# Hybrid encoder layer, one core: mLSTM gates and values beside the second HGRN pair, queries and keys behind it

## The chip, the cores and the metric

The kernel runs on one core of one Trainium2 chip. The metric is the time of one execution on the device in microseconds (us). The core's engines are named as the profile names them: PE (TensorE, matrix multiplication) with PEld (its weight loads), DVE (VectorE), ACT (ScalarE), POOL (GpSimd) and SP (SyncE, which issues most of the DMAs). Each engine works through its own queue of instructions in order; engines wait for each other by semaphores.

## What is computed

One encoder layer over 512 tokens of width 1024, in float32. Its first part, where the change lies, projects the normalised tokens once to 4624 columns and feeds four HGRN heads and four mLSTM heads of 128 columns each, both scanned forward and backward:

```python
(h_q, h_f_fwd, h_f_bwd, h_i, h_g,
 m_q, m_k, m_v, m_o,
 m_ig_fwd, m_ig_bwd, m_fg_fwd, m_fg_bwd) = split_cols(proj, IN_SPLITS)
...
o_h = hgrn2_scan(q_h, k_fwd, v_h, lf_fwd) + flip_seq(hgrn2_scan(flipped ...))
hgrn_out = head_rmsnorm(o_h, hgrn_g) * silu(h_g)
qk = silu(centred_dwconv(concat(m_q, m_k), conv_w, conv_b))        # width 5
...
h_m = mlstm_scan(q_m, k_m, v_m, ig_fwd, lfg_fwd) + flip_seq(mlstm_scan(flipped ...))
mlstm_out = head_rmsnorm(h_m, mlstm_g) * sigmoid(m_o)
x = x + concat(hgrn_out, mlstm_out) @ w_out
x = x + cross_attention(rmsnorm(x), rmsnorm(mem), ...)             # 256 memory tokens
x = x + relu(rmsnorm(x) @ w_up) ** 2 @ w_down
return rmsnorm(x, norm_final)
```

## The kernel before

Every projection of float32 values is made of three fp32r matmuls (`mm3`, L235 to L238): each operand is split into a high part (ACT copies it, L232) and a low part (DVE subtracts, L233), and high x high, high x low and low x high are added in PSUM. A block of weights, 128 x 1024, is loaded by SP into one of three `st` tiles, split into `wh` and `wl` (three tiles each), and used for 24 matmuls. The order of the blocks is the list SEQ (`_split_order`), and the splits run two blocks ahead of their use.

Projections are generators that emit a matmul group and then call `tick()` (L189), which gives one step to one of the running chains; `rate[0]` is how many steps a tick gives. `proj_d` ticks after every 12 matmuls, `proj_t` after 12 (two tiles). So chains are woven between the projection matmuls of PE's queue. The final order on each engine is made by a scheduler that knows priorities; the weight splits have a high one.

The chains around the change:

- `hgrn_pair(p)` (L359): two HGRN heads. It goes through seven levels (1, 2, 4 to 64). At each, PE computes 32 small score matmuls (L384), then DVE updates queries (L476), keys (L479) and gates (L483) of both heads and takes the scores into the matrix under a mask (L414), and ACT combines keys (L393). The next level's scores need these. After a level the chain yields `pace[0]` times, so that many ticks go by before the next. Behind the levels come L430 and L431 (products across 128 tokens), L443 and L445, and the values (L454).
- `head_out` (L486), the norm of a head: squares on ACT (L492), mean on DVE (L172), power -0.5 on POOL (L174), product on DVE (L494), then four transposes on PE (L501), the gate (L502) and a split.
- `qk_proj(p)` (L726): the projection of two heads' queries and keys, and for each of the four tiles the convolution (`conv_evac`): ACT adds the bias (L639), DVE multiplies and adds five taps (L643, four of L645), ACT takes the sigmoid (L647), DVE multiplies (L650).
- `mlstm_chain(h)` (L653): per direction a row broadcast on PE (L659), DVE adds a mask (L662), ACT writes ten exponentials of 128 x 128 (L669); then four score matmuls in full fp32 (L673), DVE multiplies (L676, L678), and the sums over tokens (L688) with the reciprocals and scalings (L694 to L701); then `head_out`.

The exponential and the sigmoid lie in different tables of ACT; where the queue changes between them, an ACT_TABLE_LOAD stands in it.

The main program projects the first pair's columns and starts it, projects the second pair's beside it, ends the first pair's levels, starts the second pair, and projects beside that: queries and keys of the first two mLSTM heads, mLSTM values (`mv_proj`, 3584), output gates (`gate_proj`, 4096 and 4352). Then the memory tokens are normed, transposed and split (L780, L783, L784), the second two heads' queries and keys are projected, and the mLSTM chains run beside the memory's keys and values (blocks of 256 columns) and the start of the output projection.

Of the kernel before, what the change touches and what calls it, by code (L numbers as in the profile page):

```python
# [33 lines left out]
V_MQK, V_MO, V_GATE = 40, 48, 52  # L34
# [11 lines left out]
def _split_order():  # L46
    def d(m, c0, n):
        return [("d", m, 0, c0 + P * i) for i in range(n)]

    def t(m, k0, c0, n=4):  # L50
        return [("t", m, k0 + 2 * i, c0) for i in range(n)]

    seq = t("in", 0, 1536) + [("d", "gate", 0, 0)]
    for g in (0, 512, 1024, 2048):
        seq += d("in", g, 2)
    for g in (0, 512, 1024):
        seq += d("in", g + 256, 2)
    seq += d("in", 2304, 2) + d("in", 2560, 2) + d("in", 3072, 2)
    seq += t("in", 0, 3584) + d("in", 4096, 2) + d("in", 4352, 2)
    seq += d("in", 2816, 2) + d("in", 3328, 2)  # L60
    seq += d("kv", 0, 8) + t("kv", 0, 1024) + t("kv", 0, 1536)
    seq += t("out", 0, 0) + t("out", 0, 512)
    seq += d("xq", 0, 8)
    seq += t("xo", 0, 0) + t("xo", 0, 512)
    for f in range(4):
        for j in range(4):
            seq += d("up", 1024 * f + P * j, 1) + d("up", 1024 * f + P * (j + 4), 1)
        seq += [("t", "down", 8 * f + 2 * g + k, 0) for g in range(2) for k in (0, 4)]
        seq += [("t", "down", 8 * f + 2 * g + 4, 512) for g in range(2)]
    seq += [("t", "down", 8 * f + 2 * g, 512) for f in range(4) for g in range(2)]  # L70
    return seq


SEQ = _split_order()
SIDX = {key: i for i, key in enumerate(SEQ)}
NSTREAM = len(SEQ) - 8
# [3 lines left out]
def trunk(ctx: ExitStack, tc: tile.TileContext, x, mem, wpk, vec, cst, lmask, rmask, rows, out):  # L80
# [12 lines left out]
    def T(tag, w, bufs, dt=F32):  # L93
        return (sb if w == 516 else big).tile([P, w], dt, tag=tag, name=nm(tag), bufs=bufs)
# [4 lines left out]
    def smb():  # L99
        return pss.tile([P, 512], F32, tag="sm", name=nm("sm"))  # L100

    def tiny(w):
        return sb.tile([P, w], F32, tag=f"tiny{w}", name=nm("tiny"), bufs=2 if w == 8 else 6)
# [9 lines left out]
    RG = lambda: T("rg", 1024, 1)  # L113
# [56 lines left out]
    def rstd_of(ss, w, n):  # L170
        ms = tiny(w)
        v.tensor_scalar(out=ms, in0=ss, scalar1=1.0 / n, scalar2=EPS, op0=ALU.mult, op1=ALU.add)  # L172
        r = tiny(w)
        gp.tensor_tensor(out=r, in0=ms, in1=nh.to_broadcast([P, w]), op=ALU.pow)  # L174
        return r, ms
# [11 lines left out]
    def tick1():  # L187
        if chains:
            turn[0] += 1  # L189
            g = chains[turn[0] % min(2, len(chains))]  # L190
            try:
                next(g)
            except StopIteration:
                chains.remove(g)
# [5 lines left out]
    def until_scored(p):  # L200
        while p not in scored:
            tick1()
# [46 lines left out]
    def proj_d(mat, c0, xs, n=512, count=2):  # L249

        for j in range(count):
            wh, wl = weights(("d", mat, 0, c0 + P * j))
            ps = mmb()
            for k in range(8):
                z = slice(k * P, k * P + P)
                mm3(ps[:, :n], wh[:, z], wl[:, z], xs[k][0], xs[k][1], k == 0, k == 7)
                if k == 3:
                    tick()
            yield ps
            tick()  # L260
# [65 lines left out]
    for t, ps in proj_t("in", 0, 1536, xs):  # L326
        d = VV()
# [306 lines left out]
    def conv_evac(h, isk, ps):  # L634
        c = (4 if isk else 0) + h
        pad = T2()
        gp.memset(pad[:, 0:2], 0.0)
        gp.memset(pad[:, 514:516], 0.0)
        sc.activation(pad[:, 2:514], ps, AF.Identity, bias=vc[:, V_MQK + c:V_MQK + c + 1])  # L639
        acc = T2()  # L640
        a = acc[:, 0:512]
        cw = lambda j: vc[:, V_CW + j * 8 + c:V_CW + j * 8 + c + 1]
        v.tensor_scalar(out=a, in0=pad[:, 0:512], scalar1=cw(0), scalar2=vc[:, V_CB + c:V_CB + c + 1], op0=ALU.mult, op1=ALU.add)  # L643
        for j in range(1, 5):
            v.scalar_tensor_tensor(out=a, in0=pad[:, j:j + 512], scalar=cw(j), in1=a, op0=ALU.mult, op1=ALU.add)  # L645
        sg = pad[:, 0:512]
        sc.activation(sg, a, AF.Sigmoid)  # L647
        if not isk:
            mq[h] = YT1(F32)
        v.scalar_tensor_tensor(out=mq[h][:, isk * 512:isk * 512 + 512], in0=a, scalar=KSCALE if isk else 1.0,  # L650
                               in1=sg, op0=ALU.mult, op1=ALU.mult)
# [56 lines left out]
    pace = [2]  # L708
# [7 lines left out]
    def gate_proj(c0, bcol, silu, buf=G4):  # L716
        gt = buf()
        for j, ps in enumerate(proj_d("in", c0, xs)):
            g = gt[:, j * 512:j * 512 + 512]
            b = vc[:, bcol + j:bcol + j + 1]  # L720
            sc.activation(g, ps, AF.Sigmoid, bias=b)
            if silu:
                v.scalar_tensor_tensor(out=g, in0=ps, scalar=b, in1=g, op0=ALU.add, op1=ALU.mult)
        return gt

    def qk_proj(p):  # L726
        for isk in range(2):
            for j, ps in enumerate(proj_d("in", 2560 + 512 * isk + 256 * p, xs)):
                conv_evac(2 * p + j, isk, ps)
                yield  # L730

    def hgrn_gate(p):
        gt = gate_proj(2048 + 256 * p, V_G + 2 * p, True)
        for j in range(2):
            hst[2 * p + j]["gate"] = gt[:, j * 512:j * 512 + 512]

    def hgrn_start(p):
        chains.append(hgrn_pair(p))

    def mlstm_start(p, gt):  # L740
        for j in range(2):
            chains.append(mlstm_chain(2 * p + j, gt[:, j * 512:j * 512 + 512]))
# [6 lines left out]
    hgrn_proj(1)  # L749
    hgrn_gate(1)  # L750
    until_scored(0)
    hgrn_start(1)
    list(qk_proj(0))
    rate[0] = 2
    mv_proj()
    rate[0] = 1
    mo0 = gate_proj(4096, V_MO, False, RG)
    mo1 = gate_proj(4352, V_MO + 2, False)

    mt = [A4(), A4()]  # L760
    for t in range(2):
        a = mt[t]
        nc.sync.dma_start(out=a, in_=mem[t * P:t * P + P, :])
        s2_ = tiny(2)
        for c in range(2):
            jk = smb()
            sc.activation(jk, a[:, c * 512:c * 512 + 512], AF.Square, accum_out=s2_[:, c:c + 1])
        ss = tiny(1)
        v.tensor_tensor(out=ss, in0=s2_[:, 0:1], in1=s2_[:, 1:2], op=ALU.add)
        r, _ = rstd_of(ss, 1, D)  # L770
        v.tensor_scalar(out=a, in0=a, scalar1=r, scalar2=None, op0=ALU.mult)
    until_scored(1)
    mlstm_start(0, mo0)
    memT = [A4(F32R) for _ in range(4)]
# [19 lines left out]
    for c in range(2):  # L794
        for t, ps in proj_t("kv", 0, 1024 + 512 * c, ms, 2):
            d = A4(F32R)
# [106 lines left out]
    for h in range(4):  # L903
        qd[h] = []
        for ps in proj_d("xq", 256 * h, x2):
            d = YT1()
# [278 lines left out]
```

## Time and profile before

| | |
|---|---|
| Time, median of 3 runs | 861.98 us (861.76 to 862.46) |
| The profiled execution | 861.91 us, of it 860.1 us in the span of the profile |
| PE busy | 840.4 us (98%), 4438 matmuls |
| PEld busy | 693.8 us (81%) |
| DVE busy | 566.6 us (66%), 996 instructions |
| ACT busy | 423.7 us (49%), 773 instructions |
| POOL busy | 67.4 us (8%) |
| Mean DMA rate | 132 GB/s |

The profile counts an engine as busy from the start to the end of an instruction; matmuls overlap one another, so that one of 512 columns counts 390 to 398 ns, though the next one starts about 0.23 us later. A wait of PE is therefore read in the timeline, from where one matmul starts to where the next one does. "PEclk" is the TensorE clock that was granted, as a share of full speed. The windows view gives busy time and clock for one stretch after another, the groups by line give the price of one instruction, and the chain that ended last names, at each step back from the end, what released it.

### The profile page before, as it was taken

What the parts mean: (1) busy time and instruction counts of PE and PEld (TensorE: products, weight loads), DVE (VectorE), ACT (ScalarE), POOL (GpSimd) and SP (SyncE); (2) the same over time, 40 slices, a digit from 0 to 9 for tenths busy, and PEclk for the clock granted to TensorE, in tenths of its full rate; (3) what the DMA queues carried; (4) which work ended last, traced back from release to release, by engine and by line L of the source; (5) the groups of instructions that cost most, each with busy time, mean ns of one, the idle gap of its engine ahead of it and who ended that gap; (6) DMA issues with size and microseconds to landing.
All of it is one profiled execution on the core that took longest, in us unless ns stands there. A gap on an engine that the chain in (4) does not pass through costs nothing.

```text
span 860.1 us, 11677 instructions
## 1 busy us (share of the span) xinstructions
PE 840.4 (98%) x4438; PEld 693.8 (81%) x4438; DVE 566.6 (66%) x996; ACT 423.7 (49%) x773; POOL 67.4 (8%) x114
## 2 busy tenths in 40 slices
PE   7999999998999999999999999999999999999995
PEld 5888788887987987888888887888888888888884
DVE  5558874599347987654545446676667656856675
ACT  5336454445558576454443346553454344434544
POOL 1000000100010000100001200003101210220001
PEclk9999999999999999999999999999999999999998
DMA  7332223122152232452213852348935993698322
GB/s 265 123 119 75 73 80 136 46 94 76 50 147 74 99 123 99 158 135 98 74 50 110 206 149 76 97 130 229 282 118 127 275 259 99 173 284 203 123 50 98
DMA packets 32682, 113.62 MB, mean 132 GB/s; under 512 B 3761, under 2 KB 3889, under 8 KB 32626
## 3 DMA queue, kind: packets, MB, share of 16 engines
q1 hardware_dynamic: 23120, 78.84, 26.9%
q0 software_dynamic: 9216, 33.56, 17.7%
q8 instruction: 35, 0.57, 0.3%
q10 hardware_dynamic: 290, 0.47, 0.2%
q14 instruction: 21, 0.17, 0.1%
HBM read 110.76 MB, written 2.10 MB: 131 GB/s over the span
## 4 chain that ended last, share of the span: by engine, by line
PE 85%; issue 6%; DVE 5%; DMA 1%; ACT 1%; POOL 1%; POOLq 0%; ACTq 0%; DVEq 0%
PE mm L236 19%; PE mm L237 19%; PE mm L238 18%; PE sm L1059 5%; PE sm L1060 5%; PE sm L1061 5%; PE sm L688 2%; PE sm L673 2%; PE sm L454 2%; DVE wl L233 1%; PE sm L384 1%; PE mm L1060 1%; PE mm L1061 1%; PE mm L1059 1%; DVE a L479 1%
## 5 line engine op out<-in xcount | busy, mean ns | idle before, releaser
L232 ACT ACTIVATE wh<-st 128x1024 fp32r<-128x1024 f32 x133 | 141.1, 1061 | 223.2 <-PE mm L237 118.8
L233 DVE TENSOR_TENSOR wl<-st,wh 128x1024 fp32r<-128x1024 f32 x133 | 162.7, 1223 | 106.8 <-ACT wh L232 101.7
L236 PE MATMUL mm<-xT,wh 128*128 128x512 f32 x544 | 216.0, 398 | 0.0
L237 PE MATMUL mm<-xT,wh 128*128 128x512 f32 x544 | 213.2, 392 | 0.4 <-DVE xT L836 0.4
L238 PE MATMUL mm<-xT,wl 128*128 128x512 f32 x544 | 212.3, 390 | 0.0
L237 PEld LDWEIGHTS mm<-xT,wh 128*128 128x128 f32 x544 | 102.2, 188 | 22.9 <-DVE xT L836 2.0
L236 PEld LDWEIGHTS mm<-xT,wh 128*128 128x128 f32 x544 | 102.2, 188 | 22.2 <-issue 0.7
L238 PEld LDWEIGHTS mm<-xT,wl 128*128 128x128 f32 x544 | 102.1, 188 | 21.3 <-issue 0.2
L951 POOL DMA_DIRECT2D as<-in_wpk x48 | 36.5, 770 | 312.0 <-DVE wl L233 187.2
L1017 DVE SCALAR_TENSOR_TENSOR t<-mm,rg 128x512 f32<-128x512 f32 x32 | 22.1, 691 | 55.1 <-PE mm L238 55.0
L236 PE MATMUL mm<-wh,yT 128*128 128x512 f32 x128 | 50.6, 395 | 0.0
L238 PE MATMUL mm<-wh,yT 128*128 128x512 f32 x128 | 50.4, 394 | 0.0
L237 PE MATMUL mm<-wl,yT 128*128 128x512 f32 x128 | 50.4, 393 | 0.0
L1059 PE MATMUL sm<-wh,yT 128*128 128x512 f32 x128 | 49.8, 389 | 0.0
L1060 PE MATMUL sm<-wl,yT 128*128 128x512 f32 x128 | 49.8, 389 | 0.0
L1061 PE MATMUL sm<-wh,yT 128*128 128x512 f32 x128 | 49.8, 389 | 0.0
L232 ACT ACTIVATE wh<-as 128x1024 fp32r<-128x1024 f32 x24 | 25.5, 1062 | 33.3 <-PE sm L1061 23.7
L233 DVE TENSOR_TENSOR wl<-as,wh 128x1024 fp32r<-128x1024 f32 x24 | 29.4, 1226 | 13.7 <-ACT wh L232 13.7
L174 POOL TENSOR_TENSOR tiny<-tiny,misc 128x4 f32<-128x4 f32 (+1 forms) x14 | 11.9, 850 | 282.5 <-DVE tiny L172 282.5
L990 DVE TENSOR_TENSOR vv<-vv,sm 128x512 f32<-128x512 f32 x48 | 31.0, 680 | 1.2 <-PE sm L1061 1.2
L236 PEld LDWEIGHTS mm<-wh,yT 128*128 128x128 f32 x128 | 24.1, 188 | 5.3 <-DVE a L233 0.5
L232 ACT ACTIVATE yT<-t 128x512 fp32r<-128x512 f32 x32 | 19.8, 630 | 17.0 <-DVE t L1034 16.5
(275 smaller groups left out, 1510.5 us busy)
## 6 DMA issues: line engine op xcount, KB each, us to landing
st<-in_wpk SPq DMA_DIRECT2D x133, 512.0 KB, 3.3
as<-in_wpk POOLq DMA_DIRECT2D x48, 512.0 KB, 7.2
gate<-in_wpk POOLq DMA_DIRECT2D x16, 512.0 KB, 7.1
as<-in_x SPq DMA_DIRECT2D x4, 512.0 KB, 6.3
vv<-in_x SPq DMA_DIRECT2D x8, 256.0 KB, 4.2
out<-vv SPq DMA_DIRECT2D x7, 256.0 KB, 2.3
a<-in_mem SPq DMA_DIRECT2D x2, 512.0 KB, 5.1
t<-in_rows SPq DMA_DIRECT2D x2, 256.0 KB, 6.1
```

The source lines that it names most:

```text
L232: sc.activation(dst_hi, src, AF.Copy)
L233: v.tensor_tensor(out=dst_lo, in0=src, in1=dst_hi.bitcast(F32), op=ALU.subtract)
L236: pe.matmul(ps, lhsT=ah, rhs=bh, start=first, stop=False)
L237: pe.matmul(ps, lhsT=ah, rhs=bl, start=False, stop=False)
L238: pe.matmul(ps, lhsT=al, rhs=bh, start=False, stop=last)
L454: pe.matmul(ps[:, t * P:t * P + P], lhsT=A[j][:, s * 512 + t * P:s * 512 + t * P + P], rhs=vh[s][:, h * P:h * P + P], start=(s == 0), stop ...
L951: gp.dma_start(out=dst, in_=wpk[idx], **kw)
L990: v.tensor_tensor(out=z, in0=z, in1=ps, op=ALU.add if sign > 0 else ALU.subtract)
L1017: v.scalar_tensor_tensor(out=y, in0=ps, scalar=0.0, in1=rrow[:, 0:512], op0=ALU.max, op1=ALU.mult)
L1059: pe.matmul(ps, lhsT=ah, rhs=bh, start=new, stop=False, **fl)
L1060: pe.matmul(ps, lhsT=ah, rhs=bl, start=False, stop=False, **fl)
L1061: pe.matmul(ps, lhsT=al, rhs=bh, start=False, stop=end and k == 1, **fl)
```

## The change

In SEQ the weights of the output gates (4096), the values and the second output gates (4352) come before the queries and keys of the first two heads. In the main program `pace[0]` becomes 3 before the second pair starts; the first output gates are projected before the values, and the projection of queries and keys moves behind the norm of the memory, just before the end of the second pair is asked for and the first mLSTM chains start. No instruction of PE or DVE is added or removed. ACT has eleven table loads in place of nine. Behind L59 the lines of the new kernel are one higher.

```diff
-    seq += d("in", 2304, 2) + d("in", 2560, 2) + d("in", 3072, 2)
-    seq += t("in", 0, 3584) + d("in", 4096, 2) + d("in", 4352, 2)
+    seq += d("in", 2304, 2) + d("in", 4096, 2)
+    seq += t("in", 0, 3584) + d("in", 4352, 2)
+    seq += d("in", 2560, 2) + d("in", 3072, 2)
...
     until_scored(0)
+    pace[0] = 3
     hgrn_start(1)
-    list(qk_proj(0))
+    mo0 = gate_proj(4096, V_MO, False, RG)
     rate[0] = 2
     mv_proj()
     rate[0] = 1
-    mo0 = gate_proj(4096, V_MO, False, RG)
     mo1 = gate_proj(4352, V_MO + 2, False)
...
         v.tensor_scalar(out=a, in0=a, scalar1=r, scalar2=None, op0=ALU.mult)
+    list(qk_proj(0))
     until_scored(1)
     mlstm_start(0, mo0)
```

The first place is DVE's queue in the levels of the second pair (`hgrn_pair(1)`, called pair 2 in what follows). `a` are queries, keys and gates of the pair, `as` the score matrix, `t` the convolution's tiles, `wl` the low part of a weight block. Before:

```order
L645 SCALAR_TENSOR_TENSOR t_221_1530<-t_220_1526,vc,t_221_1530 128x512
L645 SCALAR_TENSOR_TENSOR t_227_1573<-t_226_1569,vc,t_227_1573 128x512
L645 SCALAR_TENSOR_TENSOR t_221_1530<-t_220_1526,vc,t_221_1530 128x512
L645 SCALAR_TENSOR_TENSOR t_227_1573<-t_226_1569,vc,t_227_1573 128x512
L479 TENSOR_TENSOR a_146_976<-a_146_976,a_145_975 128x2x128x2
L233 TENSOR_TENSOR wl_1696<-st_1617,wh_1695 128x1024
L650 SCALAR_TENSOR_TENSOR yT_1385<-t_221_1530,t_220_1526 128x512
L645 SCALAR_TENSOR_TENSOR t_227_1573<-t_226_1569,vc,t_227_1573 128x512
L483 TENSOR_TENSOR a_145_975<-a_145_975 128x256
L476 TENSOR_TENSOR a_196_1352<-a_196_1352,a_152_1038 128x2x128x2
L650 SCALAR_TENSOR_TENSOR yT_1458<-t_227_1573,t_226_1569 128x512
L479 TENSOR_TENSOR a_153_1039<-a_153_1039,a_152_1038 128x2x128x2
```

Now, two levels on in the same pair:

```order
L477 TENSOR_TENSOR a_196_1352<-a_196_1352,a_145_975 128x2x16x16
L480 TENSOR_TENSOR a_146_976<-a_146_976,a_145_975 128x2x16x16
L477 TENSOR_TENSOR a_197_1353<-a_197_1353,a_152_1038 128x2x16x16
L484 TENSOR_TENSOR a_145_975<-a_145_975 128x32
L480 TENSOR_TENSOR a_153_1039<-a_153_1039,a_152_1038 128x2x16x16
L415 COPY_PREDICATED as_1354<-lm,sm_1670 128x512
L484 TENSOR_TENSOR a_152_1038<-a_152_1038 128x32
L629 TENSOR_TENSOR vv_1702<-mm_1450,t_210_1446 128x4x128
L234 TENSOR_TENSOR wl_1716<-st_1650,wh_1715 128x1024
L629 TENSOR_TENSOR vv_1711<-mm_1451,t_210_1446 128x4x128
L480 TENSOR_TENSOR a_146_976<-a_146_976,a_145_975 128x2x8x32
L477 TENSOR_TENSOR a_196_1352<-a_196_1352,a_145_975 128x2x8x32
```

The taps and products of the convolutions (L645, L650) no longer stand between the updates; the additions of the values' bias (now L629) do.

The second place is ACT's queue in the first two mLSTM heads, around a table load for the sigmoid of a convolution; `as` are the exponentials, `wh` the high part of a weight block. Before:

```order
L669 ACTIVATE as_2213<-sm_2287,bd 128x128
L647 ACT_TABLE_LOAD
L647 ACTIVATE t_328_2240<-t_329_2244 128x512
L669 ACT_TABLE_LOAD
L669 ACTIVATE as_2213<-sm_2287,bd 128x128
L232 ACTIVATE wh_2399<-st_2344 128x1024
L669 ACTIVATE as_2213<-t_339_2289,bd 128x128
L669 ACTIVATE as_2213<-sm_2287,bd 128x128 x3
L669 ACTIVATE as_2213<-t_339_2289,bd 128x128
```

Now, the last two of the seven loads of these two lines:

```order
L233 ACTIVATE wh_2629<-st_2581 128x1024
L670 ACTIVATE as_2381<-sm_2382,bd 128x128 x2
L670 ACTIVATE as_2381<-t_354_2384,bd 128x128
L670 ACTIVATE as_2381<-sm_2382,bd 128x128 x2
L670 ACTIVATE as_2381<-t_354_2384,bd 128x128
L670 ACTIVATE as_2381<-sm_2382,bd 128x128
L670 ACTIVATE as_2381<-t_354_2384,bd 128x128
L648 ACT_TABLE_LOAD
L648 ACTIVATE t_355_2408<-t_356_2412 128x512
L670 ACT_TABLE_LOAD
L670 ACTIVATE as_2381<-t_368_2453,bd 128x128
L233 ACTIVATE wh_2700<-st_2633 128x1024
```

The sigmoids of the convolutions now stand between exponentials at more places: by the two mLSTM lines (L647 and L669, now L648 and L670) there are seven loads, before five. Ahead of the first sigmoid of this piece, between two weight splits, there are eight exponentials, behind it a load, one exponential and the next split.

On PE, the last group of ten L688 stands before 48 projection matmuls and then the last L501 in the old order, with the other head's L501 after 36 of them; in the new order 15 projection matmuls stand between the last L688 and the last L501. Behind the scores of the seven levels of pair 2 stand 36, 53, 15, 11, 14, 3 and 0 projection matmuls before the next piece of that pair in the old order, and 24, 12, 24, 12, 24, 36 and 36 in the new.

## Rows read from the trace of the kernel before

**Rows 1.** Windows: us, PE, PEld, DVE, ACT, POOL busy, PEclk, DMA share, GB/s.

```profile
190.00:200.00 10.00, 10.00 (x97) 7.93 (x95) 10.00 (x18) 3.48 (x5) 0.00 (x0) 1.00 0.40 132
210.00:220.00 10.00, 7.54 (x49) 7.00 (x50) 8.20 (x17) 6.81 (x17) 0.00 (x0) 0.83 0.17 54
```

**Rows 2.** Timeline of PE, end of pair 2: start, us, what [idle before <-releaser].

```profile
210.95 0.69 PE L384 MATMUL sm<-a,t 128*64 128x64 f32 x16 [1.05 <-ACT t L393]
213.15 0.77 PE L430 MATMUL sm<-a,a 128*128 128x128 f32 x2 [1.51 <-DVE a L479]
...
216.53 1.03 PE L443 MATMUL sm<-a,a 128*128 128x256 f32 x4
```

**Rows 3.** Timeline of PE, the same matmuls in the first pair.

```profile
134.16 0.38 PE L430 MATMUL sm<-a,a 128*128 128x128 f32 x2
...
134.82 0.39 PE L431 MATMUL sm<-a,a 128*128 128x128 f32 x2
```

**Rows 4.** Timeline of DVE, one level of pair 2, first and last.

```profile
195.30 0.63 DVE L483 TENSOR_TENSOR a<-a 128x256 f32<-128x256 f32 x1
...
199.17 0.41 DVE L483 TENSOR_TENSOR a<-a 128x128 f32<-128x128 f32 x1
```

**Rows 5.** DVE's groups by line: busy us, mean ns, idle before.

```profile
L645 DVE SCALAR_TENSOR_TENSOR t<-t,vc,t 128x512 f32<-128x512 f32 x32 | 23.0, 746 | 0.2
```

**Rows 6.** Timeline of PE, projection matmuls between two levels of pair 2.

```profile
204.18 0.39 PE L238 MATMUL mm<-wh,xT 128*128 128x512 f32 x1
...
206.92 0.39 PE L238 MATMUL mm<-wh,xT 128*128 128x512 f32 x1
207.24 0.69 PE L384 MATMUL sm<-a,as 128*64 128x64 f32 x16
```

**Rows 7.** Timeline of PE, matmuls of 256 columns behind the first L501.

```profile
306.98 0.63 PE L501 MATMUL sm<-cs,t 128*128 128x128 f32 x4 [0.43 <-ACT t L700]
...
308.04 0.28 PE L236 MATMUL mm<-a,wh 128*128 128x256 f32 x1
...
310.67 0.28 PE L237 MATMUL mm<-a,wh 128*128 128x256 f32 x1
```

**Rows 8.** Timeline of all engines, the norm of a head of pair 2.

```profile
230.08 0.60 ACT L457 ACTIVATE t<-sm 128x512 f32<-128x512 f32 x1 [4.13 <-PE sm L454]
...
233.32 0.69 DVE L494 TENSOR_TENSOR t<-t,tiny 128x512 f32<-128x512 f32 x1 [1.12 <-POOL tiny L174]
```

**Rows 9.** Timeline of ACT, exponentials and a table load.

```profile
268.31 1.28 ACT L647 ACT_TABLE_LOAD   x1
269.60 0.63 ACT L647 ACTIVATE t<-t 128x512 f32<-128x512 f32 x1
...
271.81 1.05 ACT L232 ACTIVATE wh<-st 128x1024 fp32r<-128x1024 f32 x1
...
276.08 0.40 ACT L669 ACTIVATE as<-t,bd 128x128 f32<-128x128 f32 x1 [0.71 <-DVE t L662]
...
278.47 0.42 ACT L669 ACTIVATE as<-t,bd 128x128 f32<-128x128 f32 x1
```

**Rows 10.** Timeline of all engines, the last sums of an mLSTM head.

```profile
342.08 2.39 PE L688 MATMUL sm<-vv,as 128*128 128x129 f32 x20
...
343.48 1.23 DVE L233 TENSOR_TENSOR wl<-st,wh 128x1024 fp32r<-128x1024 f32 x1 [0.59 <-ACT wh L232]
...
345.28 0.14 DVE L694 TENSOR_SCALAR tiny<-sm 128x2 f32<-128x2 f32 x1
...
349.15 0.69 DVE L494 TENSOR_TENSOR t<-t,tiny 128x512 f32<-128x512 f32 x1 [1.18 <-POOL tiny L174]
```

**Rows 11.** Timeline of PE, score matmuls in full fp32.

```profile
326.28 4.02 PE L673 MATMUL sm<-yT 128*128 128x512 f32 x9
```

**Rows 12.** The chain that ended last: start, us, what.

```profile
299.09 1.11 PE sm L688 x10
...
310.95 0.60 PE sm L501 x4
```

## The prediction

> **What bounds the kernel now.** I read the windows of 10 us first, then the timeline of each engine where TensorE (PE) is not full, then the chain of waits, and last the groups by line for prices. PE is the bound: the profiled run takes 861.91 us, of which 860.1 us is the span, and PE is busy 840.4 us of that. The median of the runs shown is 861.98 us, 0.07 us above the profiled one, so a sum made against 861.91 stands for the median as it is. What a change can win is therefore PE's idle time, and what it can lose is new idle time or a lower clock.
>
> The reader is to see in [rows 1] that one stage before 400 us is different: from 190 us VectorE (DVE) is busy 10.00 of 10.00 us, and in the window from 210 us PE falls to 7.54 of 10 with a granted clock of 0.83. This is the end of the second HGRN pair. In [rows 2] its last levels show the stall: the second half of the scores of level 64 starts at 210.95 after 1.05 us of idle, the first L430 at 213.15 after 1.51 us, which ended with a DVE update (L479). Then the sixteen small matmuls of L430 and L431 take from 213.15 to 216.53, 0.21 us each. In the first pair the same matmuls run at 0.11 us ([rows 3]: eight from 134.16 to 134.82 plus two more steps, 0.88 us). So the granted clock stands at its lower level, 1.2 instead of 2.4 GHz, after these two waits, and that costs 3.38 - 1.77 = 1.6 us more. Stall and clock together: 1.05 + 1.51 + 1.6 = 4.2, with the few tenths between the rows 4.3 us.
>
> The cause is DVE's queue. One level takes 195.30 to 199.17, 3.9 us of DVE ([rows 4]), and four convolutions, each with four L645 (746 ns busy each, some 0.66 us from start to start; [rows 5], eight convolutions make its 32) and three more instructions, 3.7 us, stand in the same queue. PE in the meantime has run ahead in its own order: between the last levels it has only 14, 3 and 0 projection matmuls of 0.228 us ([rows 6]: thirteen of the fourteen from 204.18 to 206.92, then the next level at 207.24), far less than 3.9 us. Those of 256 columns, which the mLSTM stretch has, take 0.12 us ([rows 7]: 308.04 to 310.67, 23 of them).
>
> **The change, part by part.** *Order of projections and three steps per level.* The mLSTM output gates (4096, 4352) and values (3584) now run beside pair 2, the q/k projections behind. The gates cost DVE nothing but the weight split, the values four short additions. Per level PE has 24, 12, 24, 12, 24, 36 and 36 projection matmuls, mean 24 or 5.5 us, where DVE wants 3.9 us and a weight split (1.1 us) per 24. The two steps of 12 matmuls (2.7 us plus 1.2 us of scores) stand behind steps of 24, from which DVE has a lead of about 1 us. I cost the stall at nothing: minus 4.3 us. If that cover is gone, it comes back (rival E). The weight stream follows the new order in SEQ, as many loads, in the order of use; SP's queue has no other transfer moved in front of them, since the residual loads come behind. On GpSimd the powers of the norms move with their chains.
>
> *What is behind the pair.* The q/k convolutions (DVE, 4 x 3.7 us) and their sigmoids (ScalarE, ACT) now stand next to the head-norm of the pair, the memory transposes and the first two mLSTM heads. Nothing of PE's work is more or less; the question is which of its waits are new. I went through the orders of PE, ACT and DVE with start-to-start durations of rows. Five waits come out.
>
> W1, memory transposes. From the end of the last L454 the chain is copy, four squares, L172, power on GpSimd and product: 230.08 to 233.32 and 0.6 us more ([rows 8]), 3.9 us. Behind it on DVE stand a convolution's last product and the first two lo-splits, 1.4 us, for which the transposes' bank waits: 5.3 us. PE has 16 transposes and 14 projection matmuls, about 4.2 us: 1.05 us new.
>
> W2, exponentials of heads 0 and 1. ACT must write, between the end of PE's second memory-key block and the release of the banks that PE wants: a weight split 1.0, eight exponentials, a table load, a sigmoid, a table load, an exponential, a split (1.05 us busy), eight exponentials. From [rows 9]: the load takes 1.28 us and the sigmoid starts 1.29 us after it (268.31, 269.60), ten exponentials take 276.08 to 278.89, 0.28 each. So 1.0 + 2.2 + 1.28 + 0.6 + 1.28 + 0.3 + 1.0 + 2.2 = 9.9 us. PE in that time has 24 matmuls of 256 columns (2.9 us), ten L688 (twenty in the trace, 2.39 us busy, 2.1 from start to start, [rows 10]) and two fp32 L673 (each is two in the trace of 0.43, nine in 4.02, [rows 11]), 1.7 us: 6.7 us. New: 3.1, I take 3.0 us, in two pieces of 1.2 and 1.8.
>
> What the row on the load shows is a switch of 1.29 us from start to start. The Trainium skill, page "ScalarE: Activation LUTs", section "What ACT_TABLE_LOAD costs", gives about 1283 ns for the load and 1380 ns for a drain, 2.66 us per switch; its rule in the section "Table sets: the hidden batching unit" is to batch calls by set, against which this change goes (seven switches by the two mLSTM lines in place of five). The trace agrees with the load and shows no drain: 0.01 us stand between load and sigmoid. By the page's figure the sum would be 2 x 1.37 = 2.7 us higher.
>
> W3, transposes L501 of head 0. Before, the last L688 of head 0 ended at 299.09 + 1.11 = 300.20 and its L501 started at 306.98, 6.8 us later ([rows 7, 12]). In the new order PE has L673 (1.7), ten L688 (2.1) and eleven short matmuls (1.3) in between: 5.15 us, new 1.6 us. The waits that stood here, 0.43 at 306.98 and 0.16 at 310.95 (310.67 + 0.12), go: minus 0.6.
>
> W4, L501 of head 1. ACT stands between with two splits and ten exponentials, 10.4 us by the same prices, against 8.9 us of PE; its counterpart before waited the 0.16 us at 310.95 ([rows 12]). Between 0 and 1.5, I take 0.7, near the middle, since neither row is nearer.
>
> W5, start of the output projection. The last L688 is now followed by 15 projection matmuls, 3.4 us, before its L501; before, 48. The chain L694 to L494 takes 345.28 to 349.84, with 0.2 us ahead 4.8 us; measured from the end of the L688 at 344.23 it is 5.6, since a weight split (343.48) stood ahead on DVE ([rows 10]). In the new order no split stands there: 4.8 - 3.4 = 1.4, up to 2.3.
>
> Sum: 861.91 - 4.3 - 0.6 + 1.05 + 3.0 + 1.6 + 0.7 + 1.4 = 864.76, **864.8 us**. The bounds of these terms give 863.2 to 866.3.
>
> **The rivals.** B, on the other side: W2 to W4 don't come. Mechanism: ACT and DVE get ahead, in the mLSTM stretch, because the splits of the weights that I let wait for PE's slot are done early, so exponentials start a block earlier. For it: before, loads and exponentials at 268 to 279 us delayed PE by nothing ([rows 9]); against it: there 24 matmuls of 512 columns, 5.5 us, stood where now 2.9 us stand. It would give 861.91 - 4.9 + 1.05 + 1.4 = 859.5. It decides when less than 4.9 us of new waits remain; below that the change is faster.
>
> C: half of the new waits, 3.9 to 5.2 us of 7.75, are hidden by one another, as one idle spell of PE lets ACT and DVE catch up before the next. Then 861.91 - 4.9 + 3.9 to 5.2: 860.9 to 862.2, no change that can be told.
>
> D: after W2, whose two pieces follow each other within some 3 us as the two waits at 210 and 213 did, the clock falls to 1.2 GHz as there [rows 2], for 1.6 us: 866.4; after W5 too: 868.0.
>
> E: the change doesn't do what it says: with rate 2 in the values DVE still falls behind at the steps of 12 matmuls, and 1 to 4.3 us of the stall stay: 865.8 to 869. Against it: no convolution is left in that queue.
>
> F: each switch costs 2.66 us, as the page has it: 867.5. The row on the load speaks against it.
>
> **How the numbers follow.** About 0.2%, 1.7 us, is what a measurement of this kernel can tell from no change. Chances: forecast 0.37 (863.2 to 866.3), B 0.20, C 0.20, D 0.16, E 0.05, F 0.02. Faster (below 860.3): B's 0.20 and 0.01 of C, should a little more be hidden. Within 0.2% (to 863.7): 0.18 of C and 0.04 of the forecast. Slower: the rest, 0.57. The range from 858.6 to 867.6 leaves out the fast end of B (0.08) and the slow ends of D and E (0.10).
>
> **What would show it.** In the profile after: no idle time ahead of the last levels' scores and L430 (about 185 to 220 us), clock 1.00 there; PE waits ahead of L780, L674, L688 and both L501 between 225 and 290 us with ACT's exponentials and GpSimd's power as what ended them; a wait of over 1 us ahead of the last L501 in the output projection; seven table loads by the two mLSTM lines. The prediction is wrong if PE stays full between 240 and 300 us, or if DVE is still saturated at the levels. If the sum of waits is right and the time is 1.6 us longer, it is D.

## The result and the profile after

The changed kernel takes 863.45 us against 861.96 us before (medians of 15 runs each), a ratio of 1.0025 with a 95% interval of 1.0015 to 1.0036. One of the fifteen executions of the changed kernel took 1415 us at a granted clock of 0.56 and is left out of the ratio; without it the median is 863.38 us. The profiled execution takes 863.6 us, its span is 861.8 us, 1.7 more than before. PE is busy 838.8 us there, 1.6 less, so PE idles 861.8 - 838.8 = 23.0 us where it idled 860.1 - 840.4 = 19.7 us: 3.3 us more idle time and 1.6 us less work at the low clock make the 1.7 us.

The windows of 10 us of the changed kernel, columns as in [rows 1]. The window at 210 us, the stall of before, is full and at full clock; six others lack 0.4 us or more:

```profile
190.00:200.00 10.00, 10.00 (x81) 7.85 (x79) 9.95 (x19) 3.42 (x6) 0.00 (x0) 1.00 0.16 54
210.00:220.00 10.00, 10.00 (x61) 8.41 (x58) 7.51 (x15) 6.74 (x18) 1.27 (x6) 1.00 0.24 68
240.00:250.00 10.00, 9.60 (x62) 7.86 (x60) 7.14 (x13) 6.32 (x21) 2.03 (x2) 1.00 0.48 154
250.00:260.00 10.00, 9.55 (x48) 7.95 (x49) 5.75 (x12) 7.28 (x17) 0.27 (x4) 1.00 0.16 57
290.00:300.00 10.00, 7.18 (x44) 5.40 (x45) 7.86 (x26) 7.72 (x28) 0.00 (x0) 1.00 0.16 53
300.00:310.00 10.00, 9.06 (x77) 8.81 (x76) 6.87 (x27) 3.68 (x11) 1.03 (x1) 1.00 0.01 2
310.00:320.00 10.00, 9.14 (x65) 7.84 (x63) 6.73 (x10) 9.91 (x32) 1.01 (x1) 1.00 0.48 159
360.00:370.00 10.00, 8.92 (x53) 7.52 (x52) 5.97 (x17) 3.53 (x9) 1.01 (x1) 1.00 0.48 157
```

What PE waited for between 150 and 380 us in the changed kernel (total us, times, longest):

```profile
PE sm L502 <- DVE t L495: 2.9, 3, 1.1
PE sm L689 <- ACT as L670: 1.6, 1, 1.6
PE sm L674 <- DVE as L679: 1.3, 1, 1.3
PE sm L782 <- DVE a L786: 0.8, 1, 0.8
```

Together these are 6.6 us. Before, the same view of 150 to 380 us has three lines, the 1.51 and 1.05 us of [rows 2] and the 0.43 of [rows 7], 3.0 us. The sixteen L431 and L432 run at full clock now. The places can be read one by one in PE's timeline: start, us, instruction, idle before it and what ended that:

```profile
250.45 0.44 PE L782 MATMUL sm<-cs,a 128*128 128x128 f32 x2 [0.80 <-DVE a L786]
...
291.19 1.12 PE L674 MATMUL sm<-yT 128*128 128x512 f32 x2 [1.26 <-DVE as L679]
...
293.94 2.50 PE L689 MATMUL sm<-vv,as 128*128 128x129 f32 x20 [1.62 <-ACT as L670]
...
302.63 0.66 PE L502 MATMUL sm<-cs,t 128*128 128x128 f32 x4 [0.94 <-DVE t L495]
...
318.16 0.63 PE L502 MATMUL sm<-cs,t 128*128 128x128 f32 x4 [0.86 <-DVE t L495]
...
369.06 0.63 PE L502 MATMUL sm<-cs,t 128*128 128x128 f32 x4 [1.08 <-DVE t L495]
```

They stand in the order of W1 (0.80 us), the two pieces of W2 (1.26 and 1.62), W3 (0.94), W4 (0.86) and W5 (1.08). (L782 and L786 are L780 and L784 of the kernel before.) The view counts a wait from the modelled end of a matmul. Read from the start of one matmul to the start of the next, less the usual step, each of the six is 0.15 to 0.3 us longer, 7.6 us together; the expectations below, with larger numbers for the same waits (8.0 in all, 3.4 for W2), seem to count in that way.

### The profile page after: what moved, and what is told of

Read it like the earlier page. It is cut to its first block, busy times and chain, and to the rows that moved or that the text cites. A ratio compares the mean times of both kernels' runs of the same rounds, so it can differ in the third digit from the quotient of the medians.

```text
span 861.8 us, 11692 instructions
## 1 busy us (share of the span) xinstructions
PE 838.8 (97%) x4438; PEld 692.1 (80%) x4438; DVE 568.4 (66%) x996; ACT 426.2 (49%) x775; POOL 67.2 (8%) x114
## 4 chain that ended last, share of the span: by engine, by line
PE 89%; issue 5%; DVE 2%; DMA 1%; ACT 1%; POOL 1%; POOLq 0%; ACTq 0%; DVEq 0%
PE mm L237 20%; PE mm L238 20%; PE mm L239 20%; PE sm L1061 5%; PE sm L1062 5%; PE sm L1063 5%; PE sm L385 2%; PE sm L689 2%; PE sm L674 1%; PE sm L455 1%; PE mm L1062 1%; PE mm L1063 1%; PE mm L1061 1%; DMA cs<-in_cst 1%; PE sm L239 1%
## 5 line engine op out<-in xcount | busy, mean ns | idle before, releaser
L1061 PEld LDWEIGHTS sm<-wh,yT 128*128 128x128 f32 x128 | 24.0, 188 | 5.0
```

The costliest lines, as they stand in the source:

```text
L1061: pe.matmul(ps, lhsT=ah, rhs=bh, start=new, stop=False, **fl)
```

## The experiments

In all of them a theory on the cause of the waits stood against a rival. The first two take the change apart: it has two parts, the third step per level and the move of the projections. (Lines that begin with + and - are against the changed kernel, unless it says otherwise; ratios are to the kernel before.)

**The new order with two steps per level.**

```diff
-    pace[0] = 3
```

> The new order with two steps per level, as before the change. Theory T (the order alone takes the stall of the second pair away; the third step per level delays the pair's end by some 60 projection matmuls, and so the head-norms and the first mLSTM heads, and from that come the five new waits): PE's waits between 225 and 370 us, 8.0 us in the changed kernel, fall under 2 us; at the levels, now 12 matmuls (2.7 us) apart where VectorE wants 3.9, up to 2.5 us come back; time 857.5 to 860. Rival R1 (the waits come because the queries' and keys' convolutions and sigmoids now stand next to the heads, whatever the pace): at least 5 us of them stay, 861 to 864.

Measured: 862.36 us, ratio 1.0008 (0.9997 to 1.0019). Waits of PE from 150 to 380 us:

```profile
PE sm L689 <- DVE as L679: 3.0, 1, 3.0
PE sm L502 <- DVE t L495: 0.6, 1, 0.6
PE sm L781 <- DVE a L785: 0.3, 1, 0.3
```

and two windows of it:

```profile
290.00:300.00 10.00, 7.02 (x44) 6.82 (x44) 9.20 (x28) 2.81 (x5) 0.00 (x0) 0.76 0.32 106
300.00:310.00 10.00, 9.94 (x78) 9.76 (x78) 6.21 (x31) 5.38 (x22) 1.03 (x1) 0.89 0.01 2
```

Nothing is left of a stall at the levels, though only 9 to 14 projection matmuls stand between them in PE's queue. Of the five waits, W2 in its old form, W3 and W5 are gone, and W1 and W4 shrink to 0.3 and 0.6 us. But one of 3.0 us ahead of L689 has come, ended by VectorE (L679), and the clock falls behind it (0.76 and 0.89); PE's busy time, 841.6 us, is 2.8 us above the changed kernel's. So neither theory had it whole: without the third step the five waits go, shrink to some half a us or, for W2, take another form, and the move of the convolutions makes one of its own.

**The old order with three steps per level** (against the kernel before):

```diff
     until_scored(0)
+    pace[0] = 3
     hgrn_start(1)
```

> The old order with three steps per level alone. Theory T: the heads are late as in the changed kernel, so waits ahead of L673, L688 and L501 between 250 and 370 us come to 5 us or more; the stall at the last levels shrinks (17 and 19 matmuls stand there in place of 3 and 0): 863 to 866. Rival R1: the waits don't come, since queries and keys are projected early, and with the smaller stall the time is 858 to 861.

Measured: 864.37 us, ratio 1.0037 (1.0024 to 1.0050).

```profile
PE sm L501 <- DVE t L494: 2.9, 3, 1.1
PE sm L688 <- ACT as L669: 1.6, 1, 1.6
PE sm L673 <- DVE as L678: 1.3, 1, 1.3
PE sm L781 <- DVE tiny L770: 0.6, 1, 0.6
PE sm L781 <- DVE a L772: 0.2, 1, 0.2
```

L501, L688 and L673 are, by the lines of before, the L502, L689 and L674 of the changed kernel, and they wait 2.9, 1.6 and 1.3 us in both. From the first of these sums on, PE's queue has the same pieces in the same order in both kernels, to within one matmul. So W2 to W5 come from the third step alone and not from where the projections stand.

And the stall at the levels is gone here as well, with the convolutions still in VectorE's queue. What is different there is PE's queue: 20 and 19 projection matmuls stand behind the scores of the last two levels, where 3 and 0 stood. The trace of the kernel before agrees: its last instruction of a convolution ahead of the stall is this one, in VectorE's timeline, and from there to 213 us VectorE does only the levels and three weight splits.

```profile
192.34 0.69 DVE L650 SCALAR_TENSOR_TENSOR yT<-t,t 128x512 f32<-128x512 f32 x1
```

In the profiled execution of the old order with three steps the clock falls right behind the second piece of W2 (0.83 in the window from 290 us), as PE's timeline shows:

```profile
293.64 3.53 PE L688 MATMUL sm<-vv,as 128*128 128x129 f32 x15 [1.62 <-ACT as L669]
```

Fifteen L688 take 3.53 us there, 0.21 us each from start to start, where twenty took 2.50 at 293.94 in the changed kernel.

**No table loads among the exponentials.** In the changed kernel the convolution's sigmoid becomes an exponential (so that the layer computes something else there):

```diff
-        sc.activation(sg, a, AF.Sigmoid)
+        sc.activation(sg, a, AF.Exp)
```

> The changed kernel with the convolution's sigmoid replaced by an exponential (what it computes differs there), so that no table is loaded between the first heads' exponentials: eleven loads become five. Theory T2 (of the 9.9 us that ScalarE needs ahead of head 1's sums, 2.6 are two table loads on the path): the waits ahead of L674 and L689 at 291 and 294 us, 3.4 us together, fall to 1 us or less, 860.5 to 861.5. Rival R2 (the loads lie beside other waiting, ScalarE being held by weight slots or by the convolutions on VectorE): they fall by less than 0.8 us, 862.5 to 863.5.

Measured: 859.41 us, ratio 0.9970 (0.9960 to 0.9980), 4.0 us below the changed kernel and lower than theory T2 had it.

```profile
PE sm L502 <- DVE t L495: 2.0, 2, 1.1
PE sm L782 <- DVE a L786: 0.8, 1, 0.8
PE sm L502 <- DVE tiny L695: 0.5, 1, 0.5
```

The waits ahead of L674 and L689 have no line any more; W3 is 0.5 in place of 0.9 us. **The same edit in the kernel before:**

> The kernel before with the same replacement (what it computes differs there). Theory T2: the loads at 268 and 281 us lay beside 5.5 us of projection, so nothing is gained: 861.3 to 862.3. Rival R2': table loads cost PE time there too (0.5 to 1.5 us, by weight splits that come late): 860.3 to 861.3.

Measured: 861.73 us, ratio 0.9995 (0.9984 to 1.0007); nine loads become seven, and none is left among the first heads' exponentials. So taking the loads away gains nothing before and 3.3 us of PE's waits now (6.6 against 3.3). ScalarE's timeline of the changed kernel shows two loads in the path:

```profile
283.94 1.06 ACT L233 ACTIVATE wh<-st 128x1024 fp32r<-128x1024 f32 x1 [0.18 <-ACT as L670]
284.91 0.61 ACT L670 ACTIVATE as<-sm,bd 128x128 f32<-128x128 f32 x2
...
286.74 0.42 ACT L670 ACTIVATE as<-t,bd 128x128 f32<-128x128 f32 x1
287.18 1.28 ACT L648 ACT_TABLE_LOAD   x1
288.48 0.63 ACT L648 ACTIVATE t<-t 128x512 f32<-128x512 f32 x1
289.12 1.28 ACT L670 ACT_TABLE_LOAD   x1
290.42 0.40 ACT L670 ACTIVATE as<-t,bd 128x128 f32<-128x128 f32 x1
290.73 1.04 ACT L233 ACTIVATE wh<-st 128x1024 fp32r<-128x1024 f32 x1
291.67 0.35 ACT L670 ACTIVATE as<-sm,bd 128x128 f32<-128x128 f32 x1
...
293.75 0.42 ACT L670 ACTIVATE as<-t,bd 128x128 f32<-128x128 f32 x1
```

From 283.94 to 294.17 it has no gap of more than 0.03 us: a weight split, eight exponentials, load, sigmoid, load, exponential, split, nine exponentials. The prediction counted eight behind the last split, 9.9 us; the eighth ends at 293.00 + 0.89 = 293.89, 9.95 us after the start, and L689 starts at 293.94. The two loads are 2.6 of these 9.95 us. They are not all that changed in the run without them: the scheduler gave another order, with 18 short projection matmuls between the two pairs of L674 ahead of the sums where the changed kernel has 3. How much of the 3.3 us is the loads themselves and how much that order is not separated.

**Two steps per tick in the first half of the memory values**, so that the last heads end earlier:

```diff
     for c in range(2):
+        rate[0] = 2 - c
         for t, ps in proj_t("kv", 0, 1024 + 512 * c, ms, 2):
```

> The changed kernel with two steps per tick in the first half of the memory-value projection, so that the last heads' sums stand 36 projection matmuls ahead of their transposes in place of 15. Theory T3 (the wait of 1.24 us ahead of the last L502 at 369 us is only a lack of cover): it falls to 0.2 us or less and the time to about 862.3. Rival R3 (the two heads then crowd ScalarE and VectorE between 315 and 340 us): new waits of 1 to 2 us ahead of L674 or L689 there, 863 to 864.5.

Measured: 863.28 us, ratio 1.0011 (1.0002 to 1.0021).

```profile
PE sm L502 <- DVE t L495: 1.8, 2, 0.9
PE sm L689 <- ACT as L670: 1.6, 1, 1.6
PE sm L674 <- DVE as L679: 1.3, 1, 1.3
PE sm L782 <- DVE a L786: 0.8, 1, 0.8
```

L502 has two waits and 1.8 us in place of three and 2.9: W5 is gone and none took its place, as T3 had it, though the time is not the 862.3 us of T3. The median shows only 0.2 us of it, because the mean granted clock was below 0.996 in six of its ten executions and in five of fourteen of the changed kernel. Where the mean granted clock was 0.996 or more, it took 861.4 to 862.0 us, the changed kernel 862.5 to 863.6.

**A gate without a second table.** silu(a) is a/2 times (1 + tanh(a/2)). Convolution weights and bias are halved once, the key's factor goes into the bias of the exponentials:

```diff
-        sc.activation(sg, a, AF.Sigmoid)
+        sc.activation(sg, a, AF.Tanh)
...
-        v.scalar_tensor_tensor(out=mq[h][:, isk * 512:isk * 512 + 512], in0=a, scalar=KSCALE if isk else 1.0,
-                               in1=sg, op0=ALU.mult, op1=ALU.mult)
+        v.scalar_tensor_tensor(out=mq[h][:, isk * 512:isk * 512 + 512], in0=sg, scalar=1.0, in1=a, op0=ALU.add, op1=ALU.mult)
...
+        v.tensor_scalar(out=vc[:, V_CW:V_LB], in0=vc[:, V_CW:V_LB], scalar1=0.5, scalar2=None, op0=ALU.mult)
...
+        v.tensor_scalar(out=bd[:, 0:64], in0=bd[:, 0:64], scalar1=float(np.log(KSCALE)), scalar2=None, op0=ALU.add)
```

> The changed kernel with the convolution's gate as 1 + tanh of half the value, which needs no other table than the exponentials if the two functions share one; weights and bias of the convolution are halved once and the factor of the keys goes into the exponent. Eleven table loads become five. Theory T2: as with the exponential in place of the sigmoid, the 3.4 us ahead of L674 and L689 go, and 0.4 of the 1.1 ahead of the first L502: 859 to 860. Rival R2: what went there came from the order that the scheduler found and not from the loads; 862 or more.

Measured: 859.85 us, ratio 0.9979 (0.9969 to 0.9989). Five table loads are left, so the two functions do share a table, and L674 and L689 wait no more. The order is again another one (22 short matmuls between the two pairs of L674), so R2 is not excluded as a part of it. With **two steps per level** on top:

> The new order with two steps per level and the tanh of the run before. With the sigmoid, 3.2 us of wait ahead of the sums (L689) at 296 us were left, ended by VectorE, and the clock fell behind it. Theory T4 (that wait is VectorE's, four convolutions and the first heads' products in one queue, and the table loads add to it): it falls to 1 us or less, no fall of the clock, 857 to 859. Rival R4 (VectorE alone makes it, table loads have no part): 2.5 to 3.5 us stay, 861 to 862.5.

Measured: 858.18 us, ratio 0.9953 (0.9937 to 0.9970).

```profile
PE sm L503 <- DVE t L496: 1.6, 2, 1.1
PE sm L782 <- DVE a L786: 0.3, 1, 0.3
```

The wait of 3.0 us of the new order with two steps is gone with the loads, and the clock stays at 1.00 there. And with **two steps per tick in the memory values** in place of two per level:

> The tanh and the two steps per tick in the memory values together on the changed kernel. If T2 and T3 both hold, the savings add, 4.0 and 1.2 us: 858 to 859. If the two heads crowd the engines (R3), no better than the tanh alone, 859.3 or more.

Measured: 858.48 us, ratio 0.9958 (0.9944 to 0.9973): both savings add.

**The tanh in the old order with three steps per level:**

> The old order with three steps per level and the tanh: the third step without the move of projections. If the third step alone makes what the change made (stall gone, waits behind), 859.5 to 860.7, as the changed kernel with the tanh (859.85); if the move itself takes more of the stall than the third step, 861 or more.

Measured: 860.59 us, ratio 0.9991 (0.9982 to 1.0000). The third step alone makes it, as expected. The changed order with the tanh takes 859.85 us, 0.7 us less. The executions hardly overlap (859.54 to 860.54 against 860.20 to 861.08), but the two ran on different chips and the intervals of their ratios overlap: what the move of the projections brings by itself, once the third step and the tanh are there, is at most small.

**Convolutions between the pair and the heads.** Two steps per level, the first gates and the values beside the pair, then queries and keys, and the second gates behind them:

```diff
-    seq += t("in", 0, 3584) + d("in", 4352, 2)
-    seq += d("in", 2560, 2) + d("in", 3072, 2)
+    seq += t("in", 0, 3584)
+    seq += d("in", 2560, 2) + d("in", 3072, 2) + d("in", 4352, 2)
...
-    pace[0] = 3
...
     rate[0] = 1
+    list(qk_proj(0))
     mo1 = gate_proj(4352, V_MO + 2, False)
...
-    list(qk_proj(0))
     until_scored(1)
```

> Two steps per level; the first output gates and the values beside the second pair, then the queries and keys, then the second output gates (10.9 us of projection without a convolution) in front of the mLSTM heads; sigmoid as before the change. Theory T (moving the convolutions away from the pair's levels takes the stall; the waits behind come from convolutions and sigmoids among the first heads' exponentials, which here are over by then): no wait of over 0.5 us at the levels, none at L689, 857.3 to 858.5 us, without the fall of the clock. Rival R6 (levels 12 matmuls apart are too dense once convolutions follow them at once, or the heads wait whatever stands there): at least 3 us of waits, 860 or more.

Measured: 857.00 us, ratio 0.9953 (0.9940 to 0.9965), 4.6 us below the kernel before in the same session (861.58). PE's only wait from 150 to 380 us, and VectorE in four of the windows:

```profile
PE sm L502 <- ACT t L701: 0.4, 1, 0.4
```

```profile
190.00:200.00 10.00, 10.00 (x103) 8.12 (x102) 9.89 (x19) 6.55 (x13) 0.00 (x0) 1.00 0.17 54
210.00:220.00 10.00, 10.00 (x63) 8.95 (x62) 6.36 (x9) 4.18 (x8) 0.00 (x0) 1.00 0.27 87
220.00:230.00 10.00, 10.00 (x64) 8.90 (x63) 4.09 (x9) 5.16 (x20) 2.23 (x6) 1.00 0.36 116
280.00:290.00 10.00, 10.00 (x84) 9.67 (x83) 9.88 (x19) 3.54 (x6) 0.00 (x0) 1.00 0.33 108
```

The loads are back to nine, and W1, W2, W4 and W5 have no line. VectorE is as full at the levels (9.89) as in [rows 1] and PE doesn't wait, since its queue holds 9 to 14 matmuls between all of them. From the first heads' scores to their L502, PE's queue is that of the kernel before, piece for piece and down to the one wait (0.43 us there, [rows 7]), 4.8 us earlier. So this order takes the stall away and leaves the heads as they were; it does not show a new way to order the heads. **With the tanh:**

> The same with the tanh. Theory T: the loads that are left (those of the second two heads' convolutions) lie beside projections, as in the kernel before, where replacing them gave 0.2 us; so within 0.6 us of the run before. Rival: they cost 1 us or more, 856.5 or less.

Measured: 856.94 us, ratio 0.9950 (0.9937 to 0.9964), the same: here the loads lie beside other work again.

## Why the prediction was right

- **The stall goes**: as forecast, with nothing left at the levels, and with it the fall of the clock. The prediction gave two grounds, the convolutions in VectorE's queue and PE's short order (14, 3 and 0 projection matmuls against 3.9 us of VectorE per level). The second is enough: with three steps in the old order the convolutions are still there and the stall isn't. Whether the move alone, with PE's order left short, would have taken it away is not shown; no run has that.
- **The five waits**: they came at the five places. What ended them is as forecast (VectorE's lo-split for W1, ScalarE's exponentials for the second piece of W2, the product behind GpSimd's power for W3 to W5), but for the first piece of W2, which ended with VectorE's product of an exponential (L679). 0.80 for 1.05, 2.9 for 3.0, 0.94 for 1.6, 0.86 for 0.7, 1.08 for 1.4: 6.6 in place of 7.75 us. The term that was mis-sized most is W3: its chain took 6.2 us (293.94 + 2.50 = 296.44 to 302.63) in place of 6.8, while PE had 5.25 us to do in between, near the 5.15 that were counted.
- **W4 fits by luck**: at the prices of the prediction, two splits and ten exponentials are 4.9 us and not 10.4, and 0.7 was the middle of a range. In the trace 12.5 us lie between the last sums of head 1 (303.25 + 2.40 = 305.65) and its L502 at 318.16, and PE had work for 11.65 of them where 8.9 were counted.
- **Their cause**: the prediction derived them from the move of the projections. The order with its third step had them, and they were read from it, but two runs show that the third step alone makes W2 to W5. It ends the pair 84 projection matmuls later (228 stand between its first level's scores and its last values, in the changed kernel and in the old order with three steps, 144 in the kernel before), and the heads with it. The "some 60" of the expectation was too low. The size was right by the order's own rows, the reason for it was not told apart.
- **The sum**: 864.8 forecast, 863.6 in the profiled execution, 863.45 as the median, near the low end of the range. By the view's count the smaller waits make up the 1.2 us between forecast and profiled execution; read from start to start, as the terms were worked out, the waits are 7.6 us and leave most of it open. The change is 1.5 us, less than the 1.7 us that the prediction took for the least that can be told from no change; it had given a time up to 863.7 a chance of 0.22 and a longer one 0.57.
- **Rival B** (W2 to W4 don't come, 859.5) fell. Without the loads W2 is gone, W3 is halved and W4 stays, and the change would have been a gain of 2.0 to 2.5 us: B's size, not its mechanism.
- **Rival D** (a lower clock behind W2) may have come true in some executions: five of fourteen had a mean granted clock of 0.991 to 0.995 and took 864.3 to 866.0 us, the nine at 0.996 took 862.5 to 863.6. Where it fell in those five is not seen, since the profiled one is among the nine; in the profiled executions of two experiments (three steps in the old order, two steps per tick in the memory values) it fell right behind W2.
- **Rivals C and E** fell: of the 7.75 us of waits 1.15 us stayed away and not 2.5 to 3.9, and nothing of the stall is left.
- **Rival F** fell: in the rows above the sigmoid starts 1.30 us after the load (287.18 to 288.48), and the exponential behind it 1.30 us after the next one (289.12 to 290.42). So the 2.66 us per switch of the Trainium skill ("ScalarE: Activation LUTs", "What ACT_TABLE_LOAD costs") don't show in this queue. The Trainium skill's rule to batch calls by set (the same page, "Table sets: the hidden batching unit") agrees with the runs: without the switches the changed kernel takes 3.6 to 4.0 us less. That the exponential's set also holds tanh, which the same section of the Trainium skill states, agrees too: with the tanh five loads are left.

## What to carry to other kernels

Waits that vanish at one place can be paid for where the freed steps land: ask of every step that is moved which later chain now ends later, and count what PE still has in its queue there. For a chain of small levels, compare VectorE's time for a level (3.9 us here) with the projection matmuls that stand between two levels, the last ones above all. A table load of 1.28 us was free here beside a long projection, and was part of what PE waited for where the exponentials behind it were the last to come; a gate that shares the exponential's table takes the question away. In this kernel the best place for the work that fills VectorE (convolutions) was beside projections, between two chains and not beside one.

## What was not expected of the hardware

The clock does not fall in every execution of one kernel. Of 29 executions of the kernel before that ran beside the first experiments, twelve had a mean granted clock of 0.996 or 0.997 and took 860.25 to 860.8 us, seventeen 0.992 to 0.995 and 861.6 to 863.9 us, with one order of instructions. The profile of before, 861.91 us, is one in which it fell; the others have no trace. Between executions with a mean granted clock of 0.996 or more the change costs 2.7 us (863.13 against 860.45, medians), by the medians of all 1.5: the forecast, made against a profile with the fall, hit the second number. The last two kernels here, with no wait over 0.7 us from 150 to 380 us, vary by less than 1 us in five executions each. Why it falls in one execution and not in the next stays open.
